# First two projections of a decoder block from x laid out transposed, with 1/rms applied where their sums are read

## The chip, the core and the metric

One core of one Trainium2 chip runs the whole program: TensorE (PE, with its weight loads PEld), VectorE (DVE), ScalarE (ACT), GpSimd (POOL), SyncE (SP) and 16 DMA engines. The time is device microseconds of one execution; the figure quoted is the median of several runs.

## The reference, cut to what matters

512 tokens of width 1024 go through one block. Its beginning is what the change touches:

```python
def rmsnorm(x, g):
    y = xf * lax.rsqrt(jnp.mean(xf * xf, axis=-1, keepdims=True) + EPS)
    return y * g

h = rmsnorm(x, norm_mix_g)                    # (512, 1024)
proj = h @ w_in                               # 1024 -> 10 sections of 512, and 3 x 1024 gate columns
cb, cc, ch, sq, sk, sv, rq, rk, rv, rg, gate_logits = split(proj)
conv_out = cb * causal_conv3(cc * ch)
sb_out   = stick_breaking_attention(sq, sk, sv)      # 8 heads x 64
ret_out  = retention(rq, rk, rv, rg)                 # 4 heads x 128, chunks of 128 tokens
x = x + (sum of sigmoid(gates) * branch projections) @ w_o
x = x + cross-attention into 256 memory tokens
x = x + squared-ReLU MLP (4096)
return rmsnorm(x, final_g)
```

1/rms is one number per token, and `g` one per input channel. So `h @ w` equals 1/rms, per row, times `(x * g) @ w`.

## The kernel before

**Precision.** Every large matmul runs on float32r operands in three passes: each operand is split in a high part (ACT writes it, a cast) and a low part (DVE writes the source minus the high part), and `mm3` (lines 271 to 273) adds high x high, high x low and low x high in PSUM. Weights arrive as 512 KB chunks (`w_raw`, 128 x 1024, six buffers, issued on SP's queue by `Stream.load`, line 214) and are split by `parts_of` (line 111 on ACT, 112 on DVE) in `w_part` (ten buffers, two per chunk). `split` (lines 260, 261) does the same for activations; `split_scaled` does it with a factor per partition.

**Layout.** Contractions need the input channels on the partitions, so the normed `x` is kept transposed: `hT` is a `Split` of 8 channel tiles of 128 x 512 tokens, as `hT_h` and `hT_l`.

**The front.** `first_loads` (line 507 for `x`, 93 for the gain broadcast to all partitions) issues the loads. For each of the four 128-token tiles, `norm_x0` sums the squares on ACT in two halves (line 465), makes 1/rms with POOL's power (line 459) and multiplies on DVE (line 487, `xn`); `norm_T` transposes `xn` on PE in eight 128 x 128 matmuls against the identity (line 496) and splits the result into `hT`. The first projection, `sv` (the values of the stick-breaking attention, section 5, four chunks), goes token tile by token tile (`items_m` with `tok_outer`), so that a tile is projected while the next is normed. `sv_done` splits its sums into `sb_v`.

**Behind it.** All other projections read `hT`: `item_t` makes one tile of 128 output channels x 512 tokens from one weight chunk, 24 matmuls. The attention runs in 32 steps (8 heads x 4 blocks of 128 queries, the block number sets how many keys): scores (`z`, lines 599 and 600), a chain of ACT, DVE and POOL that ends in POOL's mask of `sb_suf` (line 590), then PE transposes (`aT`, line 623) and the product with `sb_v` (`o`, line 657). `fillers` are projections that the plan puts between the steps: the remaining `sq`/`sk`, the convolution's, `rq`/`rk`, and at the end `rv` (values of the retention, section 8, four token tiles of 24 matmuls), copied out by `rv_done` (line 713). The retention, the gates, the memory attention and the MLP follow.

**What sets the order.** `item` appends to a plan, which sets the program order and the weight stream; a scheduler then orders each engine's instructions when the program is built. At run time each engine, and each DMA queue, works strictly in that order.

Of the kernel before, what the change touches and what calls it, by code (L numbers as in the profile page):

```python
# [10 lines left out]
F32 = mybir.dt.float32  # L11
F32R = mybir.dt.float32r
AF = mybir.ActivationFunctionType
ALU = mybir.AluOpType
# [24 lines left out]
def trunk_kernel(ctx: ExitStack, tc: tile.TileContext, x, mem, par, rot, dqd, kdec, g_mix, g_xa, g_mem, g_mlp,  # L39
# [12 lines left out]
    def unit(name, shape=(P, 2, 512), dt=F32R):  # L52
        return upool.tile(list(shape), dt, name=name, tag="u", bufs=UNITS)
# [33 lines left out]
    pool.memset(ones, 1.0)  # L87
    prm = const.tile([P, C_N], F32, name="prm")
    kdt = const.tile([P, RH], F32, name="kdt")

    def load_g(g, eng=None):
        g_bc = unit("g_bc", (P, D), F32)
        (eng or act).dma_start(out=g_bc, in_=g.rearrange("(o d) -> o d", o=1).broadcast_to([P, D]))
        return g_bc
# [133 lines left out]
    def item(fn, *chunks):  # L228
        plan.append((chunks, fn))
# [272 lines left out]
    S = {}  # L502


    def first_loads():
        xs = S["xs"] = [unit("x", (P, D), F32) for _ in range(NT)]
        ld = lambda t: nc.sync.dma_start(out=xs[t], in_=x[t * P:(t + 1) * P, :])
        st = S["stream"]
        ld(0)
        S["g"] = load_g(g_mix, nc.sync)  # L510
        act.preload_act_table_set("natural_log_exp_and_others")
        st.load(2)
        ld(1)
        st.load(3)
        ld(2)
        ld(3)
        act.dma_start(out=prm, in_=par)
        act.dma_start(out=kdt, in_=kdec)
        S["hT"] = Split("hT", KT)

    def norm_x0(t):
        norm_begin(t, S["xs"][t])
        norm_end(t, S["xs"][t], S["g"])

    hT = lambda: S["hT"]
    item(first_loads)
    item(lambda: norm_x0(0))
    item(lambda: norm_T(0, S["hT"], 0))

    def item_t(fn, src, c, a=hT, sl=slice(None)):  # L530

# [13 lines left out]
    def sv_done(t, ps):  # L545
        for i in range(2):
            dst = S["v"][2 * i + t // 2][:, t % 2]
            split(dst[:, :, 0:SBD], dst[:, :, SBD:2 * SBD],
                  ps[:, i * 256:(i + 1) * 256].rearrange("p (a d) -> p a d", a=4))

    item(sv_alloc)
    sv = capture(lambda: items_m(w_in, sec(5), hT, sv_done, tok_outer=True))
    for t in range(NT):
        plan.append(sv[2 * t])
        if t < NT - 1:
            item(lambda t=t: norm_x0(t + 1))
        plan.append(sv[2 * t + 1])
        if t < NT - 1:
            item(lambda t=t: norm_T(t + 1, S["hT"], t + 1))

# [142 lines left out]
    def ret_tables():  # L705
        S["rot"] = unit("rot", (P, 2, 512), F32)
        S["dqd"] = unit("dqd", (P, 2, RH, P), F32)
        act.dma_start(out=S["rot"], in_=rot)
        act.dma_start(out=S["dqd"], in_=dqd)
        S["rv"] = [unit("r_v", (P, 2, 512), F32) for _ in range(2)]  # L710

    def rv_done(t, ps):
        act.copy(out=S["rv"][t // 2][:, t % 2, :], in_=ps)

    def rot_done(h, i):
        def fn(ps):
# [31 lines left out]
    def fillers():  # L748
        sqk(1), conv(0), conv(1), conv(2), sqk(2), conv(3)
        item(ret_tables)  # L750
        rqk(0), sqk(3), rqk(1), rqk(2), rqk(3)
        items_m(w_in, sec(8), hT, rv_done, tok_outer=True)

    steps = [(hd, tb) for hd in range(SBH) for tb in range(NT)]
    fill = capture(fillers)
# [468 lines left out]
    return np.stack(blocks, axis=1).transpose(0, 1, 3, 2, 4).reshape(-1, P, CW)  # L1224


def _pack_b(w):

    n = w.shape[1]
    return w.reshape(4, P, n // 256, 256).transpose(2, 1, 0, 3).reshape(n // 256, P, CW)  # L1230


def _lay_out(i):
# [6 lines left out]
    rot, dqd, kdec = _tables()  # L1240
    xkv = a["w_xkv"][0]
    return {
        "x": a["x"][0],
        "mem": a["mem"][0],
        "par": par,
        "rot": rot,
        "dqd": dqd,
        "kdec": kdec,
        "g_mix": a["norm_mix_g"][0], "g_xa": a["norm_xa_g"][0], "g_mem": a["norm_mem_g"][0],
        "g_mlp": a["norm_mlp_g"][0], "g_fin": a["final_g"],  # L1250
        "w_in": np.concatenate(secs + [_pack_t(w_in[:, 10 * W:10 * W + G7 * P])], axis=0),
        "w_gate": _pack_s(w_in[:, 10 * W + G7 * P:]),
# [36 lines left out]
```

## Time and profile before

| | |
|---|---|
| time, median of 3 runs | 1032.84 us (1031.75 to 1033.41) |
| the profiled execution | 1034.26 us, of which the instructions span 1032.5 us |
| PE / DVE / ACT / POOL busy in the span | 97% / 71% / 51% / 7% |
| DMA | 106.28 MB, mean 103 GB/s; 326 GB/s in the first fortieth of the span (26 us) |

Matmuls are pipelined, so that a record's duration is longer than its share of PE's time: the pace is read from start to start. In rows of the profile, `out<-in` names the tiles, `x8` merges eight alike, and a bracket tells how long the engine stood idle before and what ended it.

### The profile page before, as it was taken

Reading aid. Unit: us, or ns where it says so; the run is one execution under the profiler, and the core shown is the slowest. Engines: PE = TensorE matmul, PEld = TensorE weight load, DVE = VectorE, ACT = ScalarE, POOL = GpSimd, SP = SyncE. Lnnn points to the kernel's source line nnn. Section 1 sums busy time; section 2 is a strip of 40 time slices with the busy share of each in tenths; the row PEclk is TensorE's granted clock in tenths of the full one; section 3 lists DMA queues with packets and bytes.
Section 4 is the critical chain, followed back from the end, with each engine's and each line's share of the span. In section 5 each row is a group of like instructions: output and inputs, shape, how many; then the busy total and the mean of one; then the engine's idle time right before and its main releaser. Section 6 shows DMA issues by size and latency. Waiting matters only on the chain.

```text
span 1032.5 us, 13357 instructions
## 1 busy us (share of the span) xinstructions
PE 1000.0 (97%) x5060; PEld 846.0 (82%) x5060; DVE 732.8 (71%) x1092; ACT 529.3 (51%) x935; POOL 69.2 (7%) x128
## 2 busy tenths in 40 slices
PE   5999999999999999998999998999999999999996
PEld 4788888888888889997798886779888888888885
DVE  5567767866453797789796469694785695686785
ACT  5475566766532245465474346464553653553543
POOL 1111103321010000001000000000000000000000
PEclk9999999999999999999899999999999999999999
DMA  8322232213222212325445210152125115215212
GB/s 326 103 82 85 83 123 99 83 42 110 74 80 84 82 46 98 103 88 186 153 174 185 92 62 21 60 189 79 41 102 177 49 62 175 91 41 184 82 42 82
DMA packets 29873, 106.28 MB, mean 103 GB/s; under 512 B 3568, under 2 KB 3568, under 8 KB 29808
## 3 DMA queue, kind: packets, MB, share of 16 engines
q1 hardware_dynamic: 27216, 98.05, 27.4%
q0 software_dynamic: 1440, 5.24, 1.4%
q10 hardware_dynamic: 1152, 2.12, 0.6%
q8 instruction: 40, 0.66, 0.3%
q14 instruction: 25, 0.20, 0.1%
HBM read 103.31 MB, written 2.10 MB: 102 GB/s over the span
## 4 chain that ended last, share of the span: by engine, by line
PE 92%; DVE 4%; DMA 1%; ACT 1%; issue 1%; SPq 0%; POOL 0%; DVEq 0%; POOLq 0%; ACTq 0%
PE p L399 21%; PE mm L272 20%; PE mm L273 20%; PE mm L271 20%; PE p L329 5%; DVE w_part L112 1%; PE o L657 1%; PE at L496 1%; PE aT L623 1%; DMA w_raw<-in_w_in_dram 1%; PE z L599 1%; PE z L600 0%; DVE w_raw L130 0%; PE ro L804 0%; PE sc L778 0%
## 5 line engine op out<-in xcount | busy, mean ns | idle before, releaser
L112 DVE TENSOR_TENSOR w_part<-w_raw,w_part 128x1024 fp32r<-128x1024 f32 (+1 forms) x228 | 274.7, 1207 | 155.1 <-ACT w_part L111 141.3
L111 ACT CAST w_part<-w_raw 128x1024 fp32r<-128x1024 f32 (+1 forms) x228 | 236.6, 1040 | 284.4 <-PE mm L272 146.0
L272 PE MATMUL mm<-hT_l,w_part 128*128 128x512 f32 (+1 forms) x704 | 268.0, 381 | 1.7 <-DVE hT_l L261 1.7
L273 PE MATMUL mm<-hT_h,w_part 128*128 128x512 f32 (+1 forms) x704 | 267.9, 381 | 0.0
L271 PE MATMUL mm<-hT_h,w_part 128*128 128x512 f32 (+1 forms) x704 | 267.3, 382 | 0.0
L399 PE MATMUL p<-w_part,pr 128*128 128x512 f32 x864 | 206.2, 394 | 3.8 <-ACT pr L260 2.7
L399 PEld LDWEIGHTS p<-w_part,pr 128*128 128x128 f32 x864 | 162.7, 190 | 40.3 <-ACT pr L260 3.1
L272 PEld LDWEIGHTS mm<-hT_l,w_part 128*128 128x128 f32 x704 | 132.5, 188 | 25.8 <-DVE hT_l L261 1.9
L273 PEld LDWEIGHTS mm<-hT_h,w_part 128*128 128x128 f32 x704 | 132.5, 188 | 24.8
L271 PEld LDWEIGHTS mm<-hT_h,w_part 128*128 128x128 f32 x704 | 131.8, 188 | 23.7
L405 DVE TENSOR_TENSOR x<-p,x 128x512 f32<-128x512 f32 x84 | 56.8, 684 | 20.5 <-PE p L399 20.4
L399 PE MATMUL p<-w_part,pr_b 128*128 128x512 f32 x144 | 37.1, 411 | 2.4 <-ACT w_part L111 2.4
L127 DVE TENSOR_TENSOR w_raw<-w_raw 128x1024 f32<-128x1024 f32 (+1 forms) x36 | 37.5, 1042 | 0.8 <-DMA w_raw<-in_w_xo_dram 0.3
L611 DVE TENSOR_TENSOR_SCAN sb_suf<-ones,sb_e 128x128 f32<-128x128 f32 (+3 forms) x32 | 29.6, 926 | 11.3 <-POOL sb_e L590 9.6
L130 DVE TENSOR_TENSOR w_raw<-w_raw 128x1024 f32<-128x1024 f32 (+1 forms) x36 | 37.4, 1039 | 0.1
L329 PE MATMUL p<-mix_h,w_part 128*128 128x256 f32 x192 | 37.0, 283 | 0.0
L399 PEld LDWEIGHTS p<-w_part,pr_b 128*128 128x128 f32 x144 | 28.5, 199 | 9.5 <-ACT w_part L111 2.8
L329 PEld LDWEIGHTS p<-mix_h,w_part 128*128 128x128 f32 x192 | 30.9, 191 | 0.2
L465 ACT ACTIVATE xn<-x 128x512 f32<-128x512 f32 x32 | 20.0, 628 | 19.4 <-DVE x L405 16.2
L614 ACT ACTIVATE sb_suf<-sb_suf 128x128 f32<-128x128 f32 (+3 forms) x32 | 15.1, 471 | 27.7 <-DVE sb_suf L613 27.7
L329 PE MATMUL p<-hT_h,w_part 128*128 128x256 f32 x144 | 28.6, 283 | 0.4 <-ACT w_part L111 0.4
L329 PE MATMUL p<-mix_l,w_part 128*128 128x256 f32 x96 | 27.1, 283 | 0.0
(225 smaller groups left out, 1466.4 us busy)
## 6 DMA issues: line engine op xcount, KB each, us to landing
w_raw<-in_w_in_dram SPq DMA_DIRECT2D x52, 512.0 KB, 3.5
w_raw<-in_w_up_dram SPq DMA_DIRECT2D x32, 512.0 KB, 3.5
w_raw<-in_w_down_dram SPq DMA_DIRECT2D x32, 512.0 KB, 3.5
w_raw<-in_w_br_dram SPq DMA_DIRECT2D x12, 512.0 KB, 3.4
w_raw<-in_w_gate_dram SPq DMA_DIRECT2D x12, 512.0 KB, 3.5
w_raw<-in_w_o_dram SPq DMA_DIRECT2D x8, 512.0 KB, 4.0
w_raw<-in_w_xk_dram SPq DMA_DIRECT2D x8, 512.0 KB, 3.5
w_raw<-in_w_xv_dram SPq DMA_DIRECT2D x8, 512.0 KB, 3.5
```

Source lines behind the costliest of these rows:

```text
L111: act.copy(out=wh, in_=src)
L112: dve.tensor_tensor(out=wl, in0=src, in1=wh.bitcast(F32), op=ALU.subtract)
L127: dve.tensor_tensor(out=out, in0=a, in1=b, op=ALU.subtract)
L130: dve.tensor_tensor(out=out, in0=a, in1=b, op=ALU.add)
L271: te.matmul(ps, lh, rh, start=first, stop=False)
L272: te.matmul(ps, lh, rl, start=False, stop=False)
L273: te.matmul(ps, ll, rh, start=False, stop=last)
L329: te.matmul(ps[:, :256], x[:, k, :], y, start=first and k == 0 and i == 0, stop=k == 3 and i == 2, skip_group_check=True)
L399: te.matmul(acc[bank, i], x, y, start=p in ("P1", "P5", "P2") and j + k + m == 0, stop=j == 1 and k == 1 and m == 2, skip_group_check=True)
L405: dve.tensor_tensor(out=dst, in0=acc[bank, i], in1=dst, op=ALU.add)
L465: act.activation(out=dst[:, cs], in_=src[:, cs], func=AF.Square, accum_out=ss[:, i:i + 1])
L611: dve.tensor_tensor_scan(out=suf[:, :s][:, ::-1], data0=ones[:, :s], data1=e1[:, :s][:, ::-1], initial=0.0, op0=ALU.mult, op1=ALU.add)
```

## The change

The host hands over a second, transposed copy of `x` behind the first (`_pack_x`: four blocks of 128 x 1024, each two channel tiles of 512 tokens), and the gain as a column per channel tile (`gmx`, 128 x 8). From the transposed copy `xg_part` makes `xg = x * g`, split in high and low part, two channel tiles at a time. `sv` and `rv` read `xg` instead of `hT`, chunk by chunk with the four token tiles inside, so both hold four PSUM banks; `rv` moves from the end of the fillers to directly behind `sv`. The sums of squares (`x_sum`, one ACT instruction per token tile, in place) and 1/rms for all four tiles (`x_rs`) are made beside `sv`, and 1/rms is applied where the sums are read: in `sv_done` by `split_scaled`, in `rv_done` by the activation's scale. For the other projections `hT` is made without PE transposes: `x_spread` puts 1/rms of the 512 tokens on diagonals (`dg`, DVE) and one matmul against ones spreads it to all partitions (`rsp`); `hT_part` multiplies the transposed `x` with gain and `rsp` (DVE) and splits it, two channel tiles at a time. The norm loop, 32 PE transposes, their 16 splits and the gain's 512 KB broadcast go. In line numbers, lines behind 90 move by one, and those behind the front by 55.

```diff
@@ -87,6 +87,7 @@
     pool.memset(ones, 1.0)
     prm = const.tile([P, C_N], F32, name="prm")
     kdt = const.tile([P, RH], F32, name="kdt")
+    gmx = const.tile([P, KT], F32, name="gmx")
 
     def load_g(g, eng=None):
         g_bc = unit("g_bc", (P, D), F32)
@@ -502,30 +503,71 @@
     S = {}
 
 
     def first_loads():
-        xs = S["xs"] = [unit("x", (P, D), F32) for _ in range(NT)]
-        ld = lambda t: nc.sync.dma_start(out=xs[t], in_=x[t * P:(t + 1) * P, :])
+        S["xT"] = [unit("xT", (P, 2, 512), F32) for _ in range(4)]
+        S["xs"] = [unit("x", (P, D), F32) for _ in range(NT)]
+        ld = lambda t: nc.sync.dma_start(out=S["xs"][t], in_=x[t * P:(t + 1) * P, :])
+        ldT = lambda j: nc.sync.dma_start(out=S["xT"][j], in_=x[T + j * P:T + (j + 1) * P, :])
+        act.dma_start(out=gmx, in_=g_mix)
         st = S["stream"]
+        ldT(0)
+        act.preload_act_table_set("natural_log_exp_and_others")
+        st.load(1)
+        ldT(1)
+        st.load(2)
         ld(0)
-        S["g"] = load_g(g_mix, nc.sync)
-        act.preload_act_table_set("natural_log_exp_and_others")
-        st.load(2)
+        ldT(2)
+        st.load(3)
         ld(1)
-        st.load(3)
+        ldT(3)
+        st.load(4)
         ld(2)
         ld(3)
         act.dma_start(out=prm, in_=par)
         act.dma_start(out=kdt, in_=kdec)
+        S["xg"] = Split("xg", KT)
+        S["ssx"] = small.tile([P, NT], F32, name="ssx")
+    def xg_part(j):
+        for e in range(2):
+            k = 2 * j + e
+            hi, lo = S["xg"](k)
+            split_scaled(hi, lo, S["xT"][j][:, e, :], gmx[:, k:k + 1])
+    def x_sum(t):
+        xs = S["xs"][t]
+        act.activation(out=xs, in_=xs, func=AF.Square, accum_out=S["ssx"][:, t:t + 1])
+    def x_rs():
+        ms = small.tile([P, NT], F32, name="msx")
+        dve.tensor_scalar(out=ms, in0=S["ssx"], scalar1=1.0 / D, scalar2=EPS, op0=ALU.mult, op1=ALU.add)
+        S["rs"] = rstd_of(ms, NT)
+    def x_spread():
+        dg = scr("dg", (P, NT, P))
+        for t in range(NT):
+            dve.tensor_scalar(out=dg[:, t, :], in0=ident, scalar1=S["rs"][:, t:t + 1], scalar2=None, op0=ALU.mult)
+        r = S["R"] = atps("rsp")
+        te.matmul(r, ones[:, :P], dg.rearrange("p a b -> p (a b)"), start=True, stop=True)
         S["hT"] = Split("hT", KT)
 
-    def norm_x0(t):
-        norm_begin(t, S["xs"][t])
-        norm_end(t, S["xs"][t], S["g"])
+    def hT_part(j):
+        xT = S["xT"][j]
+        for e in range(2):
+            k = 2 * j + e
+            dve.scalar_tensor_tensor(out=xT[:, e, :], in0=xT[:, e, :], scalar=gmx[:, k:k + 1], in1=S["R"],
+                                     op0=ALU.mult, op1=ALU.mult)
+        split(S["hT"].h[j], S["hT"].l[j], xT)
+    xg = lambda: S["xg"]
+    item(first_loads)
+    item(lambda: xg_part(0))
 
     hT = lambda: S["hT"]
-    item(first_loads)
-    item(lambda: norm_x0(0))
-    item(lambda: norm_T(0, S["hT"], 0))
 
     def item_t(fn, src, c, a=hT, sl=slice(None)):
 
@@ -545,18 +587,31 @@
     def sv_done(t, ps):
         for i in range(2):
             dst = S["v"][2 * i + t // 2][:, t % 2]
-            split(dst[:, :, 0:SBD], dst[:, :, SBD:2 * SBD],
-                  ps[:, i * 256:(i + 1) * 256].rearrange("p (a d) -> p a d", a=4))
+            split_scaled(dst[:, :, 0:SBD], dst[:, :, SBD:2 * SBD],
+                         ps[:, i * 256:(i + 1) * 256].rearrange("p (a d) -> p a d", a=4), S["rs"][:, t:t + 1])
+    def rv_alloc():
+        S["rv"] = [unit("r_v", (P, 2, 512), F32) for _ in range(2)]
+    def rv_done(t, ps):
+        act.activation(out=S["rv"][t // 2][:, t % 2, :], in_=ps, func=AF.Copy, scale=S["rs"][:, t:t + 1])
 
     item(sv_alloc)
-    sv = capture(lambda: items_m(w_in, sec(5), hT, sv_done, tok_outer=True))
-    for t in range(NT):
-        plan.append(sv[2 * t])
-        if t < NT - 1:
-            item(lambda t=t: norm_x0(t + 1))
-        plan.append(sv[2 * t + 1])
-        if t < NT - 1:
-            item(lambda t=t: norm_T(t + 1, S["hT"], t + 1))
+    sv = capture(lambda: items_m(w_in, sec(5), xg, sv_done))
+    for j in range(3):
+        item(lambda j=j: xg_part(j + 1))
+        plan.append(sv[j])
+        item(lambda j=j: x_sum(j))
+    item(lambda: x_sum(3))
+    item(x_rs)
+    plan.append(sv[3])
+    item(rv_alloc)
+    rv = capture(lambda: items_m(w_in, sec(8), xg, rv_done))
+    plan.append(rv[0])
+    item(x_spread)
+    for j in range(4):
+        item(lambda j=j: hT_part(j))
+        plan.extend(rv[j + 1:j + 2])
 
 
 
@@ -707,10 +762,6 @@
         S["dqd"] = unit("dqd", (P, 2, RH, P), F32)
         act.dma_start(out=S["rot"], in_=rot)
         act.dma_start(out=S["dqd"], in_=dqd)
-        S["rv"] = [unit("r_v", (P, 2, 512), F32) for _ in range(2)]
-    def rv_done(t, ps):
-        act.copy(out=S["rv"][t // 2][:, t % 2, :], in_=ps)
 
     def rot_done(h, i):
         def fn(ps):
@@ -749,7 +800,6 @@
         sqk(1), conv(0), conv(1), conv(2), sqk(2), conv(3)
         item(ret_tables)
         rqk(0), sqk(3), rqk(1), rqk(2), rqk(3)
-        items_m(w_in, sec(8), hT, rv_done, tok_outer=True)
 
     steps = [(hd, tb) for hd in range(SBH) for tb in range(NT)]
     fill = capture(fillers)
@@ -1224,6 +1274,11 @@
     return np.stack(blocks, axis=1).transpose(0, 1, 3, 2, 4).reshape(-1, P, CW)
 
 
+def _pack_x(x):
+    return x.T.reshape(4, 2, P, T).transpose(0, 2, 1, 3).reshape(4 * P, 2 * T)
 def _pack_b(w):
 
     n = w.shape[1]
@@ -1240,13 +1295,13 @@
     rot, dqd, kdec = _tables()
     xkv = a["w_xkv"][0]
     return {
-        "x": a["x"][0],
+        "x": np.concatenate([a["x"][0], _pack_x(a["x"][0])], axis=0),
         "mem": a["mem"][0],
         "par": par,
         "rot": rot,
         "dqd": dqd,
         "kdec": kdec,
-        "g_mix": a["norm_mix_g"][0], "g_xa": a["norm_xa_g"][0], "g_mem": a["norm_mem_g"][0],
+        "g_mix": col(a["norm_mix_g"][0]), "g_xa": a["norm_xa_g"][0], "g_mem": a["norm_mem_g"][0],
         "g_mlp": a["norm_mlp_g"][0], "g_fin": a["final_g"],
         "w_in": np.concatenate(secs + [_pack_t(w_in[:, 10 * W:10 * W + G7 * P])], axis=0),
         "w_gate": _pack_s(w_in[:, 10 * W + G7 * P:]),
```

The first place is the DMA queue of SP at the start; `xT` is the transposed copy, and the semaphore in a bracket is the landing of an earlier transfer. Before:

```order
L507 DMA x<-in_x_dram 128x1024
L93 DMA g_bc<-in_g_mix_dram 128x1024
L214 DMA w_raw<-in_w_in_dram 128x1024 x2
L507 DMA x<-in_x_dram 128x1024
L214 DMA w_raw<-in_w_in_dram 128x1024
L507 DMA x<-in_x_dram 128x1024 [waits DMAHW0_49]
L507 DMA x<-in_x_dram 128x1024 [waits DMAHW1_49]
L214 DMA w_raw<-in_w_in_dram 128x1024 [waits DMAHW2_49]
```

and now:

```order
L514 DMA xT<-in_x_dram 128x1024
L215 DMA w_raw<-in_w_in_dram 128x1024
L514 DMA xT<-in_x_dram 128x1024
L215 DMA w_raw<-in_w_in_dram 128x1024
L513 DMA x<-in_x_dram 128x1024
L514 DMA xT<-in_x_dram 128x1024 [waits DMAHW0_49]
L215 DMA w_raw<-in_w_in_dram 128x1024 [waits DMAHW1_49]
L513 DMA x<-in_x_dram 128x1024 [waits DMAHW2_49]
L514 DMA xT<-in_x_dram 128x1024 [waits DMAHW3_49]
L215 DMA w_raw<-in_w_in_dram 128x1024 [waits DMAHW4_49]
L513 DMA x<-in_x_dram 128x1024 [waits DMAHW5_49]
L513 DMA x<-in_x_dram 128x1024 [waits DMAHW6_49]
```

The first weight chunk was the third transfer and is the second; the second chunk was fourth and is so still; the third goes from sixth to seventh, and the last tile of `x` from eighth to twelfth.

The second place is the start of ACT, with what each instruction waits for. Before:

```order
L518 DMA kdt<-in_kdec_dram 128x4
L465 ACTIVATE xn,ss<-x 128x512 [waits DMAHW0_49]
L465 ACTIVATE xn,ss<-x 128x512
L111 CAST w_part<-w_raw 128x1024 [waits DMAHW4_49]
L111 CAST w_part<-w_raw 128x1024 [waits DMAHW5_49]
L260 CAST hT_h<-at 128x2x128 [waits PE_49]
L111 CAST w_part<-w_raw 128x1024 [waits DMAHW7_49]
L260 CAST hT_h<-at 128x2x128 [waits DVE_49]
L260 CAST hT_h<-at 128x2x128 [waits PE_49]
```

and now:

```order
L112 CAST w_part<-w_raw 128x1024 [waits DMAHW2_49]
L266 ACTIVATE xg_h<-xT,gmx 128x512 [waits DMAHW1_49,DMAHW0_49]
L266 ACTIVATE xg_h<-xT,gmx 128x512
L112 CAST w_part<-w_raw 128x1024 [waits DMAHW6_49]
L266 ACTIVATE xg_h<-xT,gmx 128x512 [waits DMAHW4_49]
L266 ACTIVATE xg_h<-xT,gmx 128x512
L543 ACTIVATE x,ssx<-x 128x1024 [waits DMAHW7_49]
L266 ACTIVATE xg_h<-xT,gmx 128x512 [waits DMAHW0_49]
L266 ACTIVATE xg_h<-xT,gmx 128x512
L112 CAST w_part<-w_raw 128x1024 [waits DMAHW1_49]
L543 ACTIVATE x,ssx<-x 128x1024 [waits DMAHW2_49]
```

ACT began with the sums of `x` and alternated casts with the reading of transposes; now it begins with the first chunk's cast, and its only waits in this piece are for landings.

The third place is PE at the end of `sv`, with tile numbers (each `mm` number is one PSUM tile). Before, and behind it the first tile of `sq`:

```order
L271 MATMUL mm_354<-w_part_167,hT_h_106 128x512
L272 MATMUL mm_354<-w_part_168,hT_h_106 128x512
L273 MATMUL mm_354<-w_part_167,hT_l_110 128x512
L272 MATMUL mm_389<-hT_l_107,w_part_173 128x512
L273 MATMUL mm_389<-hT_h_103,w_part_174 128x512
L271 MATMUL mm_389<-hT_h_103,w_part_173 128x512
L272 MATMUL mm_389<-hT_l_107,w_part_173 128x512
```

and now:

```order
L272 MATMUL mm_175<-w_part_189,xg_h_116 128x512
L273 MATMUL mm_175<-w_part_190,xg_h_116 128x512
L274 MATMUL mm_175<-w_part_189,xg_l_120 128x512
L555 MATMUL rsp_345<-dg_340,ones_80 128x512
L272 MATMUL mm_312<-w_part_224,xg_h_113 128x512
L273 MATMUL mm_312<-w_part_225,xg_h_113 128x512
L274 MATMUL mm_312<-w_part_224,xg_l_117 128x512
```

Where the first tile of `sq` stood, which reads `hT`, there is now the spreading matmul and then the first token tile of `rv`, which reads `xg`; the first tile on `hT` comes 96 matmuls later.

## The prediction

> **What bounds the kernel now.** I read the page's busy shares and chain first, then who TensorE (PE) waits for, then busy time by stage, then the first 41 us row by row.
>
> ```profile
> span 1032.5 us, 13357 instructions
> PE 1000.0 (97%) x5060; PEld 846.0 (82%) x5060; DVE 732.8 (71%) x1092; ACT 529.3 (51%) x935; POOL 69.2 (7%) x128
> ...
> PE 92%; DVE 4%; DMA 1%; ACT 1%; issue 1%; SPq 0%; POOL 0%; DVEq 0%; POOLq 0%; ACTq 0%
> ```
>
> PE carries 92% of the chain that ended last; only where it stands still can time be won, or where its own work shrinks. The stages (length, then busy us and instructions of each engine):
>
> ```profile
> core 0: us, PE busy (x) PEld busy (x) DVE busy (x) ACT busy (x) POOL busy (x), PEclk, DMA share, GB/s
> 0.00:8.67 8.67, 0.00 (x0) 0.03 (x1) 1.60 (x3) 3.40 (x6) 1.75 (x9) 1.00 0.75 266
> 8.67:40.44 31.77, 29.34 (x130) 22.16 (x130) 20.97 (x39) 18.38 (x43) 3.73 (x7) 1.00 0.54 209
> 57.00:255.25 198.25, 198.25 (x968) 165.77 (x967) 145.25 (x214) 126.33 (x241) 39.27 (x77) 1.00 0.26 88
> ```
>
> PE does nothing for 8.67 us, works with gaps until 40.44, and then (third row: first to last score of the stick-breaking attention) has no gap at all. Of its waits the largest sum is for `xn`, in the front; the next is behind the attention, for the softmax of the memory attention:
>
> ```profile
> PE at L496 <- DVE xn L487: 10.0, 3, 8.7
> PE xpp L1054 <- DVE x_p L1046: 3.7, 1, 3.7
> ```
>
> Behind the attention the order of instructions is nearly the same in both kernels, so the waits there should stay. The case is the front and the attention.
>
> The front on PE (start, duration, op; x8 is eight merged transposes):
>
> ```profile
> 8.67 1.94 PE L496 MATMUL at<-ident,xn 128*128 128x128 f32 x8 [8.67 <-DVE xn L487]
> 10.61 0.80 PE L271 MATMUL mm<-w_part,hT_h 128*128 128x512 f32 x1
> 11.20 0.63 PE L272 MATMUL mm<-w_part,hT_h 128*128 128x512 f32 x1
> 11.93 0.50 PE L273 MATMUL mm<-w_part,hT_l 128*128 128x512 f32 x1
> 12.26 0.39 PE L271 MATMUL mm<-w_part,hT_h 128*128 128x512 f32 x1
> 12.49 0.39 PE L272 MATMUL mm<-w_part,hT_h 128*128 128x512 f32 x1
> 18.61 1.10 PE L496 MATMUL at<-ident,xn 128*128 128x128 f32 x8 [0.71 <-DVE xn L487]
> 31.60 0.39 PE L271 MATMUL mm<-hT_h,w_part 128*128 128x512 f32 x1
> 32.05 0.39 PE L271 MATMUL mm<-w_part,hT_h 128*128 128x512 f32 x1
> 40.44 0.39 PE L272 MATMUL mm<-hT_l,w_part 128*128 128x512 f32 x1
> ```
>
> From 32.05 to 40.44 there are 37 starts, so a full-width matmul costs (40.44 - 32.05)/37 = 0.227 us; its 0.39 us is latency. The sv projection is 96 of them, 21.8 us. At 40.44 PE has done those and one of the next tile (the row at 31.60): 40.2 us for 21.8 us of projection. The other 18.4 us are the start, 32 transposes, and stalls. The rv projection, 96 more, runs inside the gapless attention.
>
> **The change, part by part.** The measure is when PE begins the tiles that read `hT` with sv and rv both done. Before, rv comes later but costs PE the same: 40.44 - 0.23 + 21.8 = 62.0 us. Now for after.
>
> Loads. Four transfers of transposed `x` come and the broadcast gain goes, 1.5 MB more; six 512 KB transfers precede the third weight chunk instead of five.
>
> ```profile
> 4.97 0.63 ACT L465 ACTIVATE xn<-x 128x512 f32<-128x512 f32 x1 [2.88 <-DMA x<-in_x_dram]
> 5.51 0.19 ACT L465 ACTIVATION_READ_ACCUMULATOR xn<-x 128x1 f32 x1
> 7.89 1.05 ACT L111 CAST w_part<-w_raw 128x1024 fp32r<-128x1024 f32 x1 [1.59 <-DMA w_raw<-in_w_in_dram]
> 9.24 1.05 ACT L111 CAST w_part<-w_raw 128x1024 fp32r<-128x1024 f32 x1 [0.30 <-DMA w_raw<-in_w_in_dram]
> 11.79 1.05 ACT L111 CAST w_part<-w_raw 128x1024 fp32r<-128x1024 f32 x1 [1.24 <-DMA w_raw<-in_w_in_dram]
> ```
>
> ACT starts the moment these land, and they are transfers 1, 3, 4 and 6 of the SP queue: one per 1.3 us behind the first, the second therefore at about 6.5. In the new order chunk 0 is second (6.5), chunk 1 fourth (9.2), chunk 2 seventh (13.1), chunk 3 tenth (17.0), the last rows of `x` twelfth (19.5), rv's first chunk thirteenth (20.8). SP issues each when an earlier one lands, seven ahead, as before; the small column transfer `gmx` goes first on ACT's queue, where `prm` stood. What this costs PE is nothing as long as the halves below come in time.
>
> First matmul. ACT casts chunk 0 at 6.5 for 1.05, then makes the first `xg_h`, a scaled 128x512 activation.
>
> ```profile
> L603 ACT ACTIVATE sb_e<-sb_e 128x512 f32<-128x512 f32 x8 | 5.1, 635 | 0.2
> L111 ACT CAST w_part<-w_raw 128x1024 fp32r<-128x1024 f32 x5 | 5.1, 1045 | 3.1 <-DMA w_raw<-in_w_in_dram 3.1
> L112 DVE TENSOR_TENSOR w_part<-w_raw,w_part 128x1024 fp32r<-128x1024 f32 x32 | 39.0, 1222 | 12.9 <-ACT w_part L111 10.1 <-PE aT L623 2.3
> L697 DVE SCALAR_TENSOR_TENSOR cv_c<-cv_u,prm,cv_c 128x512 f32<-128x512 f32 x8 | 6.0, 745 | 0.0
> L606 DVE SCALAR_TENSOR_TENSOR sb_e<-z,sb_e 128x512 f32<-128x512 f32 x8 | 5.5, 690 | 3.6 <-ACT sb_e L604 3.5
> L713 ACT COPY r_v<-mm 128x512 f32<-128x512 f32 x4 | 2.4, 590 | 0.4 <-PE mm L273 0.4
> L459 POOL TENSOR_TENSOR rstd<-r_ve,half 128x4 f32<-128x4 f32 x4 | 4.1, 1014 | 35.3 <-DVE r_ve L813 35.3
> ```
>
> An activation with its scale from a column is bounded by 0.59 (a copy) and 0.64 (Exp); 0.62 either way puts the first matmul at 6.5 + 1.05 + 0.62 = 8.2. The second needs the chunk's low part, DVE 7.6 to 8.8: it starts at 8.9.
>
> Slow stretch. The first eight transposes take 1.94 us, eight later ones 1.10, a factor of 1.76 while the granted clock reads 1.00; the last slow start is at 11.93, 3.3 us in, and from 12.26 the pace is full. So I take 0.40 us per matmul up to 3.3 us behind the first: one at 8.2, six from 8.9 to 11.5. The remaining 89 take 20.2 us: sv ends at 31.7. Bounds: no slow matmul saves 6 x 0.17 = 1.0 us; a stretch twice as long costs 1.4 (rival 1).
>
> Do the halves come in time? Per chunk ACT has one cast, two `xg_h` and a sum of squares (1.05 + 1.24 + about 1.25, the last as one cast-length pass and a 0.19 accumulator read) = 3.5 us, DVE 1.22 + 2 x 0.75 = 2.7, PE 24 x 0.227 = 5.4. So both run ahead: chunk 3's parts are ready near 19.5 and PE wants them at 26.3. The four norm products that go had 1.28 us each on DVE:
>
> ```profile
> 17.27 1.28 DVE L487 SCALAR_TENSOR_TENSOR xn<-x,rstd,g_bc 128x1024 f32<-128x1024 f32 x1 [0.67 <-POOL rstd L459]
> 22.07 0.42 DVE L261 TENSOR_TENSOR sb_v<-mm,sb_v 128x256 fp32r<-128x256 f32 x1
> ```
>
> (the first row is what the transposes at 18.61 waited for; the second, the low half of an eviction, is used below).
>
> The 1/rms. The sums end near 21, POOL's power takes 1.0, DVE's four diagonals are in place by 25, all under sv. On PE the spreading matmul (fp32, 128x512) is new. Floor: one pass, 0.23. Ceiling: fp32 as in the retention scores.
>
> ```profile
> 274.87 0.39 PE L778 MATMUL sc<-r_qk 128*128 128x128 f32 x2
> 275.09 0.27 PE L780 MATMUL kt<-ident,r_qk 128*128 128x128 f32 x1
> ```
>
> One such product of 128 columns is two records and 0.22 us, so four times that for 512: 0.9 us. It is the same kind of operands, so I take 0.9: 32.6. Cover: none; if the diagonals were late, rv's first matmul would queue behind it.
>
> The rv projection moves to here, 21.8 us, ending at 54.4; its `r_v` eviction is a copy with a scale (0.59), and its four bank waits are for sv's evictions: eight `sb_v` halves of 0.42 us on DVE, begun at 27.8, when the first bank's sum is done. The order puts the last of them behind DVE's products with the spread 1/rms (8 x 0.69) and they end near 45, but the bank in question is claimed by the first `hT` tile only, at 54.4. The transposed norm: 8 x 0.69 + 4 x 1.22 on DVE, 4 x 1.05 on ACT, with six weight splits (7.3) in 32.6 to 54.4: 17.7 of 21.8 us on DVE. The last quarter of `hT` comes near 56, needed near 58.7, since the order runs the first three quarters of a second tile ahead of it. No wait.
>
> Sum: 62.0 - 54.4 = **7.6 us**.
>
> Attention. It loses 96 of its filler matmuls and shrinks from 198.25 to about 176.5 us. DVE loses four weight splits: 145.25 - 4.9 = 140.4, or 80% instead of 73%; ACT 126.3 - 6.6 = 119.7, 68%. So no engine becomes the bound; what could is the latency of a step, from its scores to the transposes that read its result. The tightest in the new order is a four-block step (head 6). Before:
>
> ```profile
> 229.94 0.40 PE L600 MATMUL z<-sb_k,sb_q 128*128 128x512 f32 x1
> 239.88 0.46 POOL L590 TENSOR_SCALAR_AFFINE_SELECT sb_suf<-sb_suf 128x128 f32<-128x128 f32 x1 [3.80 <-ACT sb_suf L614]
> 244.05 0.60 PE L623 MATMUL aT<-ident,sb_suf 128*128 128x128 f32 x4
> ```
>
> The result is there 10.4 us behind the scores and is read at 14.1. Between them stood 56 full-width matmuls, now 41: 14.1 - 15 x 0.227 = 10.7. It still fits, by 0.3 us. Price taken: nothing, with up to 0.5 us in each of the eight four-block steps, 4 us, as the upper bound.
>
> **The rivals.** Rival 1, the slow pace lasts longer. The transposes that stood in the slow stretch are gone, and one matmul stands alone before a 0.3 us gap. If the slow pace lasts to 8.2 + 2 x 3.3 = 14.8, (14.8 - 11.5)/0.40 = 8 more matmuls lose 0.17 us each: 1.4, giving 1026.6. Against it: at 10.61 to 11.93 PE also had gaps and yet was at full pace by 12.26. The Trainium skill ("TensorE: Matmul & The Clock Gate", Part 1) says the slow state ends after about 3.4 us of sustained activity, in a window that runs free of the kernel's start; by its worst phase, two windows, the sum would be this rival's, and by its best the forecast's. Its Part 4 says that transposes don't count as activity in the same way; by that the pace here would have become full 3.4 us behind the first matmul at 10.61, at 14.0 (an estimate from that page). The trace has it by 12.26, so the measurement decides and I keep 3.3 us behind the first PE work of any kind.
>
> Rival 2, slower: the attention's steps set their own pace. If the stage keeps its 198.25 us because each step must wait for its chain, PE idles for rv's 21.8 us and the kernel takes 1025.2 + 21.8 = 1047; it turns slower once the 32 steps wait 0.24 us each. For it: the 0.3 us above, and DVE at 80%. Against it: PE has not one wait there before, and the step shown is the tightest of the 32.
>
> Rival 3, the front doesn't gain: split and norm work move PE's waits from the transposes to `hT`. DVE's 17.7 us alternate with ACT's casts; with every handover exposed the last quarter could come 5 us later than worked out, and 5 - 2.7 = 2.3 us of it would stand on PE: 1027.5. For it: the weight splits queued ahead of that quarter wait for parts that rv's last token still reads. Against it: those reads end at about 52.
>
> **How the numbers follow.** The profiled execution took 1034.26 for its span of 1032.5; 7.6 less is 1026.7 and 1024.9. The median of the runs shown, 1032.84, lies 1.4 below that execution, so I predict 1025.2. Chances: forecast 0.65; rival 1 0.10; rival 3 0.06; the attention with 1 to 9 us of waits 0.12 (a third of it under 1030.8); rival 2 beyond its turning point 0.07. The range: below, no slow stretch (1.0) and the runs' own spread (1032.84 - 1031.75 = 1.1), 1023.1; above, 4 us of attention waits and 1 us of rival 1, 1030.2. A measurement here tells about 0.2%, 2.1 us, from no change: faster is everything below 1030.8, 0.65 + 0.10 + 0.06 + 0.04 = 0.85; same is the rest of the attention's mild case, 0.08; slower is rival 2, 0.07.
>
> **What would show it.** Right: first matmul at 8.2, sv's last near 31.7, first tile on `hT` at 54.4, no wait for `xn` in PE's list, none between there and the end of the attention, and the 3.7 us softmax wait still there. Wrong: waits of PE on `xg_l` or `w_part` below 31.7 (splits late), on `hT` behind 54 (rival 3), on `sb_suf` (rival 2), or starts 0.4 us apart up to 15 us (rival 1).

## The result and the profile after

The changed kernel takes 1027.08 us (median of 5 runs, 1026.85 to 1027.97) against 1032.84; the ratio is 0.9949 with a 95% interval of 0.9935 to 0.9964, so 5.8 us or 0.5% faster. The forecast was 1025.2 with a range of 1023.1 to 1030.2. The profiled execution took 1027.97 us, of which the instructions span 1026.3 us:

```profile
span 1026.3 us, 13274 instructions
PE 995.6 (97%) x5030; PEld 843.1 (82%) x5030; DVE 734.8 (72%) x1089; ACT 533.4 (52%) x923; POOL 64.5 (6%) x125
...
PE 93%; DVE 5%; issue 1%; ACT 1%; DMA 0%; POOL 0%; DVEq 0%; POOLq 0%; SPq 0%; ACTq 0%
```

PE's matmul count falls by 30 (32 transposes go, two records of the spreading matmul come), and its share of the chain rises by a point. The engines that PE waits for (us in total, times, longest):

```profile
PE mm L272 <- ACT xg_h L266: 7.8, 1, 7.8
PE xpp L1104 <- DVE x_p L1096: 3.7, 1, 3.7
...
PE mm L272 <- DVE r_qk L775: 1.1, 1, 1.1
```

The 10.0 us for `xn` are gone and the softmax wait of 3.7 stands, but the last row is new: a wait for the eviction of a rotary tile, `r_qk`, in the middle of the attention. (A rotary tile is a tile of `rq` or `rk`; `rot_done` reads its sums out of PSUM, with two copies of halves by ACT and one multiplication by DVE, and rotates it by position with the table `rot`.) The front, row by row on PE:

```profile
7.84 0.80 PE L272 MATMUL mm<-w_part,xg_h 128*128 128x512 f32 x1 [7.84 <-ACT xg_h L266]
8.48 0.80 PE L273 MATMUL mm<-w_part,xg_h 128*128 128x512 f32 x1
9.07 0.63 PE L272 MATMUL mm<-w_part,xg_h 128*128 128x512 f32 x1
9.50 0.63 PE L273 MATMUL mm<-w_part,xg_h 128*128 128x512 f32 x1
...
11.63 0.46 PE L274 MATMUL mm<-w_part,xg_l 128*128 128x512 f32 x1
11.93 0.39 PE L272 MATMUL mm<-w_part,xg_h 128*128 128x512 f32 x1
12.16 0.39 PE L273 MATMUL mm<-w_part,xg_h 128*128 128x512 f32 x1
...
31.65 1.02 PE L555 MATMUL rsp<-dg,ones 128*128 128x512 f32 x2
...
32.75 0.40 PE L273 MATMUL mm<-w_part,xg_h 128*128 128x512 f32 x1
...
54.32 0.39 PE L272 MATMUL mm<-hT_h,w_part 128*128 128x512 f32 x1
```

From the third on, matmuls start 0.43 us apart up to 11.63, and from 11.93 0.23 apart. The spreading matmul stands at 31.65, and the first tile on `hT` at 54.32, without a wait since the first matmul. Against the 62.0 that the kernel before would have needed for the same work, the front wins 7.7 us.

The lost part is here (PE, then what DVE and POOL do at that time; the bracket gives the idle time and its releaser):

```profile
226.30 0.39 PE L274 MATMUL mm<-hT_h,w_part 128*128 128x512 f32 x1
227.76 0.50 PE L272 MATMUL mm<-hT_h,w_part 128*128 128x512 f32 x1 [1.07 <-DVE r_qk L775]
...
225.21 0.58 ACT L773 COPY r_sw<-mm 64x512 f32<-64x512 f32 x1
...
225.55 0.96 DVE L666 TENSOR_TENSOR_SCAN sb_suf<-ones,sb_e 128x384 f32<-128x384 f32 x1
225.93 1.65 POOL L774 TENSOR_TENSOR r_sw<-r_sw,rot 128x512 f32<-128x512 f32 x1 [0.41 <-ACT r_sw L773]
...
226.54 0.56 DVE L668 TENSOR_TENSOR sb_suf<-z,sb_suf 128x384 f32<-128x384 f32 x1
...
227.02 0.68 DVE L775 TENSOR_TENSOR r_qk<-mm,rot 128x512 f32<-128x512 f32 x1
```

The next tile of PE wants the PSUM bank of a rotary tile. ACT had read that tile by 225.79, but DVE's reading of it stands in DVE's queue behind a scan and a product of a stick-breaking step, so the bank comes free at 227.7 instead of before 226.7. The tail of the kernel agrees: PE's last group of matmuls starts at 1023.72 before and 1016.94 after.

```profile
1023.72 0.84 PE L399 MATMUL p<-w_part,pr 128*128 128x512 f32 x3
```

```profile
1016.94 0.84 PE L400 MATMUL p<-w_part,pr 128*128 128x512 f32 x3
```

That is 6.8 us: 7.7 won in front, 1.07 lost to the bank, 0.2 won elsewhere (not followed up). The profiled executions differ by 6.3, since what follows that group is 0.5 longer after (8.8 us before, 9.3 now; 0.3 of it is a 1/rms that POOL begins 0.62 us behind its input in place of 0.31, the rest was not followed up). The medians differ by 5.8, since the profiled execution of before lay 1.4 over its median and that of after 0.9.

### The profile page after: what moved, and what is told of

Read it like the earlier page. It is cut to its first block, busy times and chain, and to the rows that moved or that the text cites. A ratio compares the mean times of both kernels' runs of the same rounds, so it can differ in the third digit from the quotient of the medians.

```text
span 1026.3 us, 13274 instructions
## 1 busy us (share of the span) xinstructions
PE 995.6 (97%) x5030; PEld 843.1 (82%) x5030; DVE 734.8 (72%) x1089; ACT 533.4 (52%) x923; POOL 64.5 (6%) x125
## 4 chain that ended last, share of the span: by engine, by line
PE 93%; DVE 5%; issue 1%; ACT 1%; DMA 0%; POOL 0%; DVEq 0%; POOLq 0%; SPq 0%; ACTq 0%
PE p L400 21%; PE mm L272 20%; PE mm L273 20%; PE mm L274 20%; PE p L330 5%; DVE w_part L113 1%; PE o L712 1%; PE aT L678 1%; PE at L497 1%; PE z L654 0%; DMA w_raw<-in_w_in_dram 0%; PE z L655 0%; DVE w_raw L128 0%; DVE w_raw L131 0%; PE ro L854 0%
## 5 line engine op out<-in xcount | busy, mean ns | idle before, releaser
L666 DVE TENSOR_TENSOR_SCAN sb_suf<-ones,sb_e 128x128 f32<-128x128 f32 (+3 forms) x32 | 27.4, 857 | 9.5 <-POOL sb_e L645 8.2
L272 PE MATMUL mm<-w_part,xg_h 128*128 128x512 f32 x64 | 26.4, 413 | 7.8 <-ACT xg_h L266 7.8
```

What stands on the lines that cost most here:

```text
L272: te.matmul(ps, lh, rh, start=first, stop=False)
L666: dve.tensor_tensor_scan(out=suf[:, :s][:, ::-1], data0=ones[:, :s], data1=e1[:, :s][:, ::-1], initial=0.0, op0=ALU.mult, op1=ALU.add)
```

## The experiments

Each is an edit of the changed kernel and is timed against the kernel before on the same chip. The changed kernel once more beside them, as a control:

> The changed kernel itself once more, beside the following variants, for its time and above all for the length of its slow first stretch, which was 3.6 us in the profile of before (8.67 to 12.26), 4.1 in that of the changed kernel (7.84 to 11.93), 5.5 with the first weight chunk loaded first (6.72 to 12.2) and 4.3 behind the added transposes (1.89 to 6.2). My theory: the switch to full pace does not follow the first instruction by a fixed time, so the length differs from execution to execution of the same kernel, between 3.4 and 6.8 us, and 1 us of the differences between executions comes from it. Rival, the length is fixed by the order of this kernel's first instructions: 4.1 us again, within 0.1. Time 1026.5 to 1028 us, with the attention's wait of 1.07 us for r_qk as before.

Measured: 1027.15 us (1026.88 to 1027.71), ratio 0.9945 (0.9932 to 0.9957); the bank wait of 1.1 is there again. Its slow stretch ran from 7.65 to 11.29:

```profile
7.65 0.80 PE L272 MATMUL mm<-w_part,xg_h 128*128 128x512 f32 x1 [7.65 <-ACT xg_h L266]
...
11.29 0.40 PE L274 MATMUL mm<-w_part,xg_l 128*128 128x512 f32 x1
```

3.6 us, against 4.1 in the first profile of the same kernel; more of this below.

**rv back at the end of the fillers, on hT.**

```diff
-        act.activation(out=S["rv"][t // 2][:, t % 2, :], in_=ps, func=AF.Copy, scale=S["rs"][:, t:t + 1])
+        act.copy(out=S["rv"][t // 2][:, t % 2, :], in_=ps)
...
-    item(rv_alloc)
-    rv = capture(lambda: items_m(w_in, sec(8), xg, rv_done))
-    plan.append(rv[0])
...
-        plan.extend(rv[j + 1:j + 2])
...
+        item(rv_alloc)
+        items_m(w_in, sec(8), hT, rv_done, tok_outer=True)
```

> The rv projection goes back to the end of the attention's fillers and reads hT again; all else is as in the changed kernel. My theory: rv's 21.8 us are the cover under which the transposed norm is made, so without it TensorE reaches the first tile on hT at about 32.6 and waits. The first quarter of hT needs the spread 1/rms (there at 32.6), two products of 0.69, a cast of 1.05 and a low half of 1.22 us, so it is there at about 36; the other quarters follow every 2.6 us, and a quarter feeds 12 matmuls (2.7 us) of two interleaved tiles. Waits of 3.5 to 7 us in all behind 32.6, and the attention gets its 96 filler matmuls back, so its wait for r_qk (1.1 us) goes: 1029.5 to 1033.5 us. Rival A, the move of rv does not matter and the gain is the earlier start and the transposes alone: 1026 to 1028 us, with no new wait. Rival B, the move of rv itself costs more in the attention than it hides in the front: under 1026 us.

Measured: 1034.94 us (11 runs, 1033.82 to 1039.27), ratio 1.0023 (1.0011 to 1.0035): 0.2% slower than the kernel before. PE behind the spreading matmul:

```profile
32.38 1.02 PE L555 MATMUL rsp<-dg,ones 128*128 128x512 f32 x2
35.97 0.73 PE L272 MATMUL mm<-hT_h,w_part 128*128 128x512 f32 x2 [2.57 <-ACT hT_h L261]
38.02 0.77 PE L272 MATMUL mm<-hT_h,w_part 128*128 128x512 f32 x1 [1.31 <-DVE sb_v L267]
41.90 0.80 PE L273 MATMUL mm<-hT_l,w_part 128*128 128x512 f32 x1 [3.12 <-DVE hT_l L262]
42.49 0.63 PE L274 MATMUL mm<-hT_h,w_part 128*128 128x512 f32 x1
...
46.76 0.59 PE L272 MATMUL mm<-hT_h,w_part 128*128 128x512 f32 x1
```

My theory stands in direction: the first quarter of `hT` comes at 35.97 (forecast 36), the waits sum to 7.0 us, and the attention's wait for `r_qk` is gone. Both rivals fall. The range (up to 1033.5) was missed because I had not priced what follows the waits: from 42.49 the next 11 starts are 0.43 us apart instead of 0.23, 2.2 us more. So in this order the early `rv` carries the whole gain; without it the change loses.

**hT by transposes, rv still early.**

```diff
-    item(x_spread)
+    item(hT_alloc)
...
-        item(lambda j=j: hT_part(j))
+        item(lambda j=j: hT_norm(j))
+        item(lambda j=j: norm_T(j, S["hT"], j))
```

For one token tile each, `hT_norm` makes `xn` = x * 1/rms * gain on DVE, and `norm_T` its eight transposes and their splits. Not shown: the gain's 512 KB broadcast is loaded again, and the squares go to a tile of their own, since `x` is still needed.

> As the changed kernel, with rv still early on the scaled x, but hT is made as before by norm products and 32 TensorE transposes in place of the spread matmul and the products on transposed x (one more 512 KB load, the broadcast gain). It parts the two halves of the front's gain: transposes saved, and waits saved. My theory: the transposes now stand behind rv, where nothing waits for the norm, and cost their own time, 8 for 1.10 us as in the profile of before, so 4.4 us, against 0.9 us saved for the spread matmul: 3 to 4 us slower than the changed kernel, 1030 to 1031.5 us, with the first full-width matmul on hT at about 53.5 and the transposes among the first tiles. Rival, nearly all of the gain is the waits: within 1 us of the changed kernel, 1026.5 to 1028 us. Other rival, the norm and the evictions come late behind sv and rv: over 1032 us, with waits of TensorE for xn.

Measured: 1038.89 us (1037.25 to 1040.07), ratio 1.0053 (1.0039 to 1.0067): 11.8 over the changed kernel, where I expected 3 to 4. The front took 4.4 us more, a little over the forecast: the first tile on `hT` starts at 58.76 in place of 54.32 (I had it at about 53.5, with the transposes among the first tiles; all of them came ahead of it). Not all of that is the transposes: 0.9 is the wait in the row below, for the copy of the last eight, and 0.6 a longer slow stretch in this execution, whose full pace began at 13.01 instead of 11.93. So 2.9 us are left for the transposes net of the spreading matmul. Most of the rest is one wait of PE and what follows it:

```profile
58.76 0.96 PE L272 MATMUL mm<-hT_h,w_part 128*128 128x512 f32 x3 [0.88 <-ACT hT_h L261]
...
237.41 0.80 PE L272 MATMUL mm<-hT_h,w_part 128*128 128x512 f32 x1 [6.13 <-DVE r_qk L786]
238.00 0.63 PE L273 MATMUL mm<-hT_l,w_part 128*128 128x512 f32 x1
...
241.42 0.52 PE L272 MATMUL mm<-hT_h,w_part 128*128 128x512 f32 x1
```

The same bank wait as in the changed kernel, now 6.13 us, and then eight starts 0.43 us apart, 1.6 us more. None of the theories named it. This says that the attention's wait depends on the order in which the tiles fall, and can be several times what the change paid. Why it is so long, on DVE and POOL:

```profile
233.28 0.58 ACT L784 COPY r_sw<-mm 64x512 f32<-64x512 f32 x1
...
234.09 1.26 POOL L785 TENSOR_TENSOR r_sw<-r_sw,rot 128x512 f32<-128x512 f32 x1
234.16 2.01 DVE L677 TENSOR_TENSOR_SCAN sb_suf<-ones,sb_e 128x384 f32<-128x384 f32 x1
...
236.68 0.68 DVE L786 TENSOR_TENSOR r_qk<-mm,rot 128x512 f32<-128x512 f32 x1
```

DVE's reading stands behind the step's scan here too, ACT's own copies come later (233.86), and the scan of 384 takes 2.01 us instead of 0.96.

**ScalarE copies that one tile out of PSUM**, in the variant with transposes and in the changed kernel:

```diff
+            src = ps
+            if (h, i) == (1, 1):
+                src = dst
+                act.copy(out=dst, in_=ps)
-            dve.tensor_tensor(out=dst, in0=ps, in1=S["rot"][:, 0, :], op=ALU.mult)
+            dve.tensor_tensor(out=dst, in0=src, in1=S["rot"][:, 0, :], op=ALU.mult)
```

> The variant that makes hT with 32 transposes, whose attention waited 6.13 us for the bank of the rotary tile of head 1 (key side), with ScalarE's copy of that one tile as above. My theory: the wait is one bank held by one late eviction on VectorE. ScalarE's two swapped copies of that tile end at 233.9, the added copy at 234.5, so TensorE goes on there instead of at 237.4: 2.9 us less, 1035.5 to 1036.5 us, with 3.2 us of waits left, which are ScalarE's own lateness (the copies stand behind a weight cast and an exponential). The rest of the difference to the changed kernel is 4.4 us of transposes in front of the attention. Rival: TensorE waits for the stick-breaking step as a whole, and any relief at the bank shows up again at the next tile: 1038 to 1039 us.

Measured: 1035.24 us (10 runs, 1034.38 to 1036.10), ratio 1.0019 (1.0010 to 1.0029), 3.65 us less than without the copy and just under the forecast of 1035.5 to 1036.5. PE goes on at 234.51 (forecast 234.5):

```profile
234.51 0.66 PE L272 MATMUL mm<-hT_h,w_part 128*128 128x512 f32 x1 [3.23 <-ACT r_qk L789]
```

The releaser is now ACT's copy, and 3.2 us are left, as expected; behind them, too, the starts are 0.43 us apart at first, for 3.45 us. That the bank was what PE waited for is shown. In the changed kernel:

> In the one rotary tile (head 1, key side) whose bank TensorE waited for at 226.7 us in the changed kernel, ScalarE copies the sums out of PSUM behind its two swapped copies, and VectorE's multiplication reads the copy; one ScalarE instruction of 0.59 us more. My theory: the lost 1.07 us is the bank being held by VectorE's eviction, which stands behind a scan and a subtraction of a stick-breaking step; ScalarE had its two copies done at 225.8 and is idle until 226.3, so the bank is free at 226.4, the wait goes, and 1025.9 to 1026.2 us result. Rival A: the wait moves to the next tile's bank or to the step's transposes, since VectorE is as late as before: 1027 us. Rival B: the added copy delays the step's exponentials on ScalarE and TensorE waits for those: over 1027.5 us.

Measured: 1027.32 us (1026.82 to 1029.37), ratio 0.9946 (0.9933 to 0.9960): no gain. The wait at 226.7 is gone, and another has come at the next rotary tile:

```profile
235.74 0.50 PE L272 MATMUL mm<-hT_h,w_part 128*128 128x512 f32 x1 [1.74 <-DVE r_qk L779]
...
232.00 1.29 POOL L774 TENSOR_TENSOR r_sw<-r_sw,rot 128x512 f32<-128x512 f32 x1
232.06 2.30 DVE L666 TENSOR_TENSOR_SCAN sb_suf<-ones,sb_e 128x512 f32<-128x512 f32 x1 [0.46 <-POOL sb_e L645]
```

Rival A. So I copied that tile and all that follow, `(h, i) >= (1, 1)`:

> ScalarE's copy of the sums, as in the variant with one copied tile, now for that rotary tile and all that follow it (five of eight, 0.59 us each on ScalarE). With one copied tile the wait of 1.07 us at 226.7 went, and one of 1.72 us came at 234.0, for the bank of the next rotary tile, again held by VectorE's eviction behind a scan. My theory: the wait follows whichever rotary tile VectorE still has to read out of PSUM late; with all of them copied no bank waits, TensorE runs without a gap from the first hT tile to the end of the scores as in the kernel before, and 1025.8 to 1026.3 us result. Rival A, the step sets the pace: the scan and its products are late in any case, and TensorE waits for the transposes of that step or for ScalarE's own lateness: 1027 to 1029 us, with waits on sb_suf or on r_qk from ScalarE.

Measured: 1026.21 us (6 runs, 1023.69 to 1028.37), ratio 0.9936 (0.9919 to 0.9953). No wait of PE for `r_qk` or for anything else between the first `hT` tile and the end of the scores, as my theory had it; the time lies inside its range, but the runs spread over 4.7 us and the interval overlaps that of the changed kernel. The granted clock sorts them: over the whole run it averages 0.990 in the three at 1027.7 to 1028.4 us, and 0.993 or 0.995 in the three at 1023.7 to 1024.7. The median stands between two groups, so this run alone does not tell what the copies are worth. The step as a whole does not set the pace.

**The first weight chunk ahead of the first part of x.**

```diff
-        ldT(0)
+        st.load(1)
         act.preload_act_table_set("natural_log_exp_and_others")
-        st.load(1)
+        ldT(0)
```

> The first weight chunk is loaded ahead of the first part of transposed x; nothing else is changed. In the changed kernel TensorE starts at 7.84 us, behind a chain of chunk 0 landing (6.1), its cast (1.04) and the scaled copy of x (0.72). My theory: the chunk lands first, at about 4.9, its cast ends at 6.0 while x lands at 6.1, and the first matmul starts at 6.8 to 6.9; since TensorE has no wait from there to 54 us, the whole 0.9 to 1.0 us arrives at the end: 1026.0 to 1026.3 us. Rival: the low part of the chunk or the second scaled copy of x is then the late one, the start moves but sv still ends at 31.6: 1027 us.

Measured: 1025.92 us (1025.64 to 1027.45), ratio 0.9931 (0.9920 to 0.9943). The start moved as forecast, but in the profiled execution the slow stretch was longer, and the first `hT` tile stands at 53.92, only 0.4 us earlier than in the first profile of the changed kernel and no earlier than in the control (53.91):

```profile
6.72 0.79 PE L272 MATMUL mm<-w_part,xg_h 128*128 128x512 f32 x1 [6.72 <-ACT xg_h L266]
...
12.01 0.58 PE L272 MATMUL mm<-w_part,xg_h 128*128 128x512 f32 x1
12.43 0.39 PE L273 MATMUL mm<-w_part,xg_h 128*128 128x512 f32 x1
```

So the median agrees with my number (1026.0 to 1026.3) to 0.1 us, but the trace shows that most of the 1.1 us of earlier start went into slow matmuls in that execution. Whether the time follows the start alone stays open.

**Transposes ahead of the first matmul.**

```diff
+    def warm():
+        w = atps("warm")
+        for i in range(24):
+            te.transpose(w[:, (i % 4) * P:(i % 4 + 1) * P], ident, ident)
     xg = lambda: S["xg"]
+    item(warm)
```

> 24 transposes of the identity are added on TensorE ahead of the first matmul, from about 1.9 to 6.5 us, where it otherwise does nothing; their result is read by nobody. In the changed kernel the first eight matmuls start 0.40 to 0.43 us apart against 0.227 later, though the granted clock reads 1.00, until 11.9 us, 4.1 us behind the first one. My theory: the slow pace depends on how long TensorE has been working, transposes counting as work, so the 24 take the slow pace on themselves, the matmuls run at 0.227 from the first on, 1.2 to 1.6 us are saved and 1025.5 to 1025.9 us result. Rival A: transposes do not count as work, and the matmuls are slow as before: 1027 us. Rival B: the pace is not TensorE's but that of what feeds it (the halves of x and the weights), and waits for xg_l or w_part take the place of the slow starts: 1026.5 to 1027 us.

Measured: 1026.81 us (1025.79 to 1028.11), ratio 0.9939 (0.9926 to 0.9952); PE's start:

```profile
1.89 4.99 PE L569 MATMUL warm<-ident 128*128 128x128 f32 x24 [1.89 <-POOL ident masks.py:199]
7.80 0.50 PE L272 MATMUL mm<-w_part,xg_h 128*128 128x512 f32 x1 [0.92 <-ACT xg_h L266]
8.43 0.50 PE L273 MATMUL mm<-w_part,xg_h 128*128 128x512 f32 x1
8.76 0.39 PE L272 MATMUL mm<-w_part,xg_h 128*128 128x512 f32 x1
8.99 0.39 PE L273 MATMUL mm<-w_part,xg_h 128*128 128x512 f32 x1
```

The matmuls run 0.23 apart from the third on, and the first `hT` tile stands at 52.74, 1.2 to 1.6 us earlier than in the two profiles of the changed kernel: my theory in the trace, against both rivals. In the median time only 0.3 us of it arrive, but the median span from the first to the last instruction is 1024.2 us against 1025.4 in both sets of runs of the changed kernel, 1.2 us less. The difference is that two of the five runs took 2.7 and 2.8 us beyond their span, where every run of the changed kernel took 1.7 or 1.8. Some runs of the later variants with these transposes show the same (2.2 to 2.8 us), and no run without them; why was not followed up.

**The edits together.** First the two of the front and the one copy:

> The changed kernel with three edits together: first weight chunk loaded first, 24 unread transposes of the identity ahead of the first matmul, and ScalarE's copy of the one rotary tile. My theory: the first matmul at 6.75 us and at full pace, so sv ends near 29.0 in place of 31.65 (1.1 from the start, 1.5 from the pace), and the 1.07 us of the attention's wait on top: 3.6 us under the changed kernel, 1023.3 to 1023.8 us. Rival A: with the start and the pace both better TensorE overtakes the second weight chunk or the halves of x and waits below 12 us: 1024.3 to 1025.3. Rival B: the attention's wait comes back elsewhere, as it did when other edits shifted the order: 1025 to 1029.

Measured: 1026.50 us (1024.96 to 1028.21), ratio 0.9936 (0.9924 to 0.9949). The first `hT` tile is at 51.61 as expected, but the bank wait came back at the next tile with 1.7 us, and behind it eight starts at the slow pace: rival B. Then the two edits of the front alone, and those with the five copies:

> Only the two edits of the front: first weight chunk loaded first, and 24 unread transposes of the identity ahead of the first matmul. My theory: first matmul at 6.75 at full pace, first tile on hT at 51.6 as in the combined variant (53.9 to 54.3 in the changed kernel), the attention's wait of 1.07 us as there: 2.3 to 2.7 us under the changed kernel, 1024.5 to 1025 us. Rival: what is won in front is lost behind, because weight chunks or the softmax of the memory attention come at their own time, or because another wait of TensorE brings a slow stretch that the changed kernel did not have: 1026 to 1027 us.

> The two edits of the front together with ScalarE's copy for five rotary tiles. My theory: the sum of both, with no wait of TensorE between the first matmul and the end of the scores: 1.1 us under the variant with the front alone, 1023.4 to 1023.9 us. Rival: the copies only shift the attention's wait, and this is no better than the front alone: 1024.5 to 1027 us.

Measured: the front alone 1025.89 us (6 runs, 1023.85 to 1028.21), ratio 0.9934 (0.9920 to 0.9948), between my theory and its rival; with the five copies 1023.35 us (1021.97 to 1024.04), ratio 0.9906 (0.9893 to 0.9920), at the lower end of my theory's forecast and 0.4% under the changed kernel, with intervals that do not touch. Against the front alone the intervals just meet; the runs with the same granted clock, 0.993, span 1023.1 to 1023.7 us with the front alone and 1021.3 to 1021.5 with the copies, so the copies do bring something here. Its stretch (length, then busy us and instructions of each engine) from the first `hT` tile to the retention's first scores:

```profile
51.68:260.97 209.29, 209.29 (x1021) 174.59 (x1020) 156.72 (x230) 140.72 (x262) 38.02 (x81) 1.00 0.27 91
```

PE is busy for all of the 209.29 us. This version beats both kernels.

## Why the prediction was right, and where it was off

- **Loads and start.** First matmul at 7.84 (forecast 8.2), the second at 8.48 (8.9): the chunk landed 0.4 us earlier than the spacing of 1.3 us gave (its cast began at 6.12, not 6.5). The scaled activation took 0.72 us, outside the 0.59 to 0.64 that I had called its bounds.
- **Slow stretch.** Forecast as 3.3 us from the first work to the last slow start, with `sv` ending at 31.7; measured that way it took 3.8 us (7.84 to 11.63) and `sv` ended at 31.65, the earlier start covering for it, which is luck. The step was wrong in kind, too: I took one trace's length as fixed. Measured to the first start at full pace, the stretch took 3.6 us in the kernel before, 3.6 from 7.65 in the control, 4.1 from 7.84, 5.7 from 6.72, 4.9 to 5.3 in four other variants, and from 7.62, in the kernel with one copied tile, 6.2, close to what rival 1 describes:

```profile
7.62 0.79 PE L272 MATMUL mm<-w_part,xg_h 128*128 128x512 f32 x1 [7.62 <-ACT xg_h L266]
...
13.85 0.40 PE L274 MATMUL mm<-w_part,xg_l 128*128 128x512 f32 x1
```

  The control and the changed kernel are one program, so the length differs from execution to execution. The prediction cited the Trainium skill ("TensorE: Matmul & The Clock Gate", Part 1) for a window that runs free of the kernel's start, and set it aside for a fixed 3.3 us; these rows agree with the page. Its Part 4, that transposes don't count as activity in the same way, does not hold here: 24 transposes alone brought the full pace.
- **Halves of x, diagonals, cover of hT.** No wait of PE between 7.84 and 54.32, as argued; rv's return to the fillers shows that the cover was needed, by 7.0 us of waits where it is gone.
- **Spreading matmul.** Forecast 0.9; from 31.65 to the next full-paced start at 32.75 are 1.10, of which one matmul is 0.23, so 0.87.
- **rv and the sum.** First `hT` tile forecast at 54.4, read at 54.32; gain of the front 7.6 against 7.7. That it agrees to 0.1 us is luck in part: in the four profiled executions with this front (both of the changed kernel, and those with one and with five copied tiles) the tile stands at 53.91 to 55.14.
- **Attention.** "Price taken: nothing" was the mis-sized term: 1.07 us. I had looked for the tightest place between a step's scores and the transposes that read its result, and none of those waits. What wait there is falls on a PSUM bank whose last reader stands in DVE's queue behind a step. It is inside the 4 us that I gave as the upper bound, but by a path that the prediction did not name; the copies by ACT, which take it away or move it, show that path.
- **Median.** 1.9 us over the forecast: 1.1 for that wait, 0.5 for the tail, the rest from how the two profiled executions lay to their medians. Rivals 2 and 3 did not occur.

## What to carry to other kernels

When filler work is taken out of a stage that has no gap, check not only whether each step's result is in time for its reader, but for each PSUM bank which engine reads it last and what stands ahead of that reading in the engine's queue. A reading that takes its place behind a chain of dependent work is best given to an engine that is done with the tile already, and to all tiles of the kind, since freeing one moved the wait to the next. A wait of the matmul engine may cost more than its length, because a slow stretch can follow it.

## What the runs showed that I had not expected

- After a wait of 6.13 us PE started its next matmuls 0.43 us apart for 4.0 us more, after 3.12 us for 4.9 us and after 3.23 us for 3.45 us; after 1.07 us it did not, and of two waits of 1.74 us one was followed by such starts and the other not. In the row of such a stretch (length, then busy us of each engine, then the granted clock, the first number behind POOL's) the granted clock reads 0.50, in the variant with transposes:

```profile
238.00:241.42 3.42, 3.42 (x10) 2.65 (x8) 2.62 (x4) 1.66 (x3) 1.87 (x2) 0.50 0.00 0
```

```profile
9.07:11.63 2.56, 2.56 (x7) 1.98 (x6) 2.41 (x4) 2.56 (x4) 0.00 (x0) 1.00 1.03 413
```

  The second row is the start of the changed kernel, as slow by its starts, but with 1.00: at the start of these executions that column does not show the slow pace, and the distance of the starts does.
- DVE's scan and POOL's rotary product lengthen one another, and the one that starts second pays. Scan first (225.55, POOL at 225.93): 0.96 and 1.65 us. POOL first by 0.07 us (234.09): the same scan takes 2.01, POOL 1.26. The Trainium skill ("SBUF — State Buffer", SBUF: two separate sides) says that a VectorE instruction with two inputs in SBUF and a GpSimd one that reads SBUF lock one another out for a whole instruction; the rows agree within 0.2 us of what that gives (1.26 - 0.07 + 0.96 = 2.15 for the second scan, and 0.96 - 0.38 + 1.26 = 1.84 for the first product).
